# A four-layer decoder trunk on eight cores: phase barriers removed, weights cast by DMA, attention placed inside the convolution, down-projection fused with the embedding

## The chip, the cores and the metric

One Trainium2 chip, eight cores. Each core runs the same program on one of eight sequences of 4096 tokens; there is no traffic between cores. The metric is the device time of the slowest core in microseconds (us). The chip has two dies, cores 0 to 3 and cores 4 to 7. TensorE is the engine that runs the matmuls; ScalarE, VectorE and GpSimd do the work element by element; PSUM is the memory that matmuls write to, SBUF the one that tiles lie in. An execution can fall into a slower state, in which the cores of one die or of both show a lower granted TensorE clock (the changed kernel's run of 10,140.83 us: 0.968 to 0.969 on cores 0 to 3, 0.983 to 0.985 on cores 4 to 7); runs are compared within one state, and where an experiment was run on a chip that was seldom in the fast state, its stages are compared on cores whose clock was not lowered (how, is told with the experiments).

## The reference

Four layers, width 1024, and a last RMS norm. One layer, cut to what matters:

```python
a = rms_norm(h, norm_mix_g[i])
z = a @ w_in[i]                          # 7936 columns: q, k, v, conv x/B/C, gating u|v, three gates
q, k = rotary_partial(zq), rotary_partial(zk)
ya = dilated_mixture(q, k, v)            # 12 heads of 64; three groups of 4 heads with
                                         # (window, dilation) = (128,1), (512,4), (2048,16)
yb = zb * short_conv(zc * zx, conv_w[i]) # causal, width 3
yc = spatial_gating(zs, ...)             # u * (tril(W_s) layer_norm(v) + b), chunks of 128
gates = sigmoid(zg)
m = gates[0]*(ya @ w_branch_a[i]) + gates[1]*(yb @ w_branch_b[i]) + gates[2]*(yc @ w_branch_c[i])
h = h + m @ w_out[i]
h = h + square(relu(rms_norm(h, norm_mlp_g[i]) @ w_up[i])) @ w_down[i]
h = h + sigmoid(rms_norm(h, norm_ple_g[i]) @ w_ple_gate[i]) * (p[i] @ w_ple_proj[i])
```

Attention works in blocks of 128 queries against their own and the previous block of keys of the same residue; the three groups' outputs are weighted by their softmax denominators, so the sum of exponentials is needed as well as the weighted values.

## The kernel before

Activations lie with the channel on the partitions and the token along the row; a tile is 512 tokens. A layer is eight phases, each ended by a wait of all engines for all:

```python
    def barrier(self):
        tot = dict(self.count)
        for e in ENGS:
            for k, v in tot.items():
                # ... every engine waits for the last instruction of every other, and for every DMA
                self.streams[e].append(("w", k, v))
    # ...
    for l in range(nl):
        # ...
        phase_qkv(l, aT, aR, preload=lambda: load_act(aTd, aT, aR, "aTd"))   # activations back from DRAM
        phase_conv_gates(l, aT, aR)
        phase_sgu(l, aT, aR)
        phase_attn(l)
        phase_merge(l, xT if l == 0 else hT, wts)
        phase_ffn_up(l, cT, cR, preload=lambda: load_act(cTd, cT, cR, "cTd"))
        phase_ffn_down(l, wd, rwd)
        phase_ple(l, wg, wp, rwp, m, fuse)
```

Weights come as f32 into a staging buffer and are cast to bf16 by ScalarE and VectorE in turn. Attention puts the mask into PSUM by matmuls and makes the denominators by matmuls against ones:

```python
    for (mi, ksl, vbi) in kbs:
        for ps in (psE, psO):
            e.matmul(ps[:, mi * 256:(mi + 1) * 256], lhsT=ident, rhs=maskb[:, mi, 0:256], start=True, stop=False, ...)
    # ... scores of 128 columns on top; exponential on ScalarE; then per head
            ins = e.matmul(pso[pb:pb + 64, ...], lhsT=vs[:, vbi, j * 64:(j + 1) * 64], rhs=pt[:, c0:c0 + 128], ...)
            ins = e.matmul(pso[pb:pb + 64, 256 + ...], lhsT=onesb[:, 0:64], rhs=pt[:, c0:c0 + 128], ...)
```

In the merge, the output projection of a tile follows that tile's own products and GpSimd additions. Norms of a tile are written to DRAM and read back by the next phase.

The softmax here doesn't subtract the row's maximum and nothing guards it: scores larger than these inputs give would overflow.

Of the kernel before, what the change touches and what calls it, by code (L numbers as in the profile page):

```python
# [13 lines left out]
AX = mybir.AxisListType  # L14
# [3 lines left out]
T = 512  # L18
NT = S // T
KC = D // 128  # L20
NL = 4
INW = 7936
DFF = 4096
PLE = 256
# [3 lines left out]
MASKV = -240000.0  # L28
# [3 lines left out]
C_G = 4864  # L32

ENGS = ("pe", "act", "dve", "pool", "sp")
DBG = 99

class Res:
    __slots__ = ("writers", "readers", "excl")

    def __init__(self):  # L40
        self.writers = {}
        self.readers = {}
        self.excl = False

class Prog:
    def __init__(self, nc):
        self.nc = nc
        self.streams = {e: [] for e in ENGS}
        self.count = {e: 0 for e in ENGS}
        self.seen = {e: {} for e in ENGS}  # L50
        self.semh = {}
        self.res = {}
        self.ndma = 0

    def R(self, *key):
        r = self.res.get(key)
        if r is None:
            r = self.res[key] = Res()
        return r

    def newsem(self, key):
        self.count[key] = 0
        return key

    def _deps(self, eng, reads, writes):
        deps = {}
        for r in reads:
            for k, v in r.writers.items():
                if deps.get(k, 0) < v:
                    deps[k] = v  # L70
            if r.excl:
                for k, v in r.readers.items():
                    if k != eng and deps.get(k, 0) < v:
                        deps[k] = v
        for w in writes:
            for dct in (w.writers, w.readers):
                for k, v in dct.items():
                    if k != eng and deps.get(k, 0) < v:
                        deps[k] = v
# [20 lines left out]
    def dma(self, out, in_, sem, reads=(), writes=(), q="sp"):  # L100
        self._deps(q, reads, writes)
        self.count[sem] += 16
        v = self.count[sem]
        self.streams[q].append(("o", lambda e, o=out, i=in_: e.dma_start(out=o, in_=i), sem, 16))  # L104
# [5 lines left out]
        self.ndma += 1  # L110

    def barrier(self):
        tot = dict(self.count)
        for e in ENGS:
            seen = self.seen[e]
            for k, v in tot.items():
                if k == e and e == "pe":
                    continue
                if v > 0 and seen.get(k, 0) < v:
                    self.streams[e].append(("w", k, v))  # L120
                    seen[k] = v
        for r in self.res.values():
            r.writers = {}
            r.readers = {}
# [37 lines left out]
class Arena:  # L162
    def __init__(self, nc, limit=229000):
        self.nc = nc
        self.off = 16640
        self.n = 0
        self.limit = limit

    def alloc(self, shape, dtype, name="t"):
        esz = 4 if dtype in (F32, I32) else 2  # L170
        nbytes = esz * int(np.prod(shape[1:]))
        nbytes = (nbytes + 63) // 64 * 64
        off = self.off
        self.off += nbytes
        assert self.off <= self.limit, ("SBUF arena overflow", name, self.off)
        self.n += 1
        return self.nc.alloc_sbuf_tensor_at("%s_%d" % (name, self.n), list(shape), dtype, offset=off)

    def mark(self):
        return self.off  # L180

    def reset(self, m):
        self.off = m

def build_program(nl=NL, final_norm=True, stop=99):
    nc = bass.Bass("TRN2", target_bir_lowering=False)
    P = Prog(nc)
    A = Arena(nc)
# [7 lines left out]
    xT = din("xT", [D, S])  # L196
    pT = din("pT", [NL, PLE, S])
    pos = din("pos", [1, S], I32)
    w_in = din("w_in", [NL, D, INW])
    w_a = din("w_a", [NL, 768, D])  # L200
    w_b = din("w_b", [NL, 512, D])
    w_c = din("w_c", [NL, 512, D])
    w_out = din("w_out", [NL, D, D])
    w_up = din("w_up", [NL, D, DFF])
    w_down = din("w_down", [NL, DFF, D])
    w_pg = din("w_pg", [NL, D, D])
    w_pe = din("w_pe", [NL, PLE, D])
    sgwT = din("sgwT", [NL, 4, 128, 128])
    gains = din("gains", [128, NL * 3 + 1, KC])
    convw = din("convw", [128, NL, 4, 3])  # L210
    lng = din("lng", [NL, 1, 512])
    lnb = din("lnb", [NL, 1, 512])
    sgb = din("sgb", [NL, 1, 512])
    cmat = din("cmat", [128, 4, 128])
    cmask = din("cmask", [128, 2, 512])
    invf = din("invf", [128, 1])
    outT = nc.dram_tensor("outT", [D, S], F32, kind="ExternalOutput").ap()

    hT = dscr("hT", [D, S], F32)
    cosD = dscr("cosD", [128, S], F32)  # L220
    sinD = dscr("sinD", [128, S], F32)
    qkT = dscr("qkT", [12, 128, S], BF16)
    Vd = dscr("Vd", [3, 128, 32 * 256], BF16)
    ybT = dscr("ybT", [4, 128, S], BF16)
    ycT = dscr("ycT", [4, 128, S], BF16)
    gT = dscr("gT", [24, 128, S], BF16)
    yaT = dscr("yaT", [6, 128, S], BF16)
    fT = dscr("fT", [32, 128, S], BF16)
    cTd = dscr("cTd", [KC, 128, S], BF16)
    aTd = dscr("aTd", [KC, 128, S], BF16)  # L230

    PS = [nc.alloc_psum_tensor("ps%d" % i, [128, 512], F32) for i in range(8)]
    PSR = [P.R("ps", i) for i in range(8)]
    for r_ in PSR:
        r_.excl = True

    cm = A.alloc([128, 4, 128], BF16, "cm")
    ident, rotT, onesb, trilb = (cm[:, i, :] for i in range(4))
    cmf = A.alloc([128, 4, 128], F32, "cmf")
    onesf = cmf[:, 2, :]  # L240
    maskb = A.alloc([128, 2, 512], BF16, "maskb")
    gsb = A.alloc([128, NL * 3 + 1, KC], F32, "gsb")
    cwsb = A.alloc([128, NL, 4, 3], F32, "cwsb")
    invfsb = A.alloc([128, 1], F32, "invf")
    epsb = A.alloc([128, 1], F32, "epsb")
    Rconst = P.R("const")
    base_mark = A.mark()

    cnt = {"sem": 0}

    def dsem():
        cnt["sem"] += 1
        key = "d%d" % cnt["sem"]
        if key not in P.count:
            P.newsem(key)
        return key

    _pbar = P.barrier

    def barrier():  # L260
        _pbar()
        cnt["sem"] = 0

    P.barrier = barrier

    class Slots:
        def __init__(self, n, shape, dtype, name):
            self.t = [A.alloc(shape, dtype, name) for _ in range(n)]
            self.r = [P.R(name, id(self), i) for i in range(n)]
            self.s = [dsem() for _ in range(n)]  # L270
            self.i = -1
            self.n = n

        def next(self):
            self.i = (self.i + 1) % self.n
            return self.t[self.i], self.r[self.i], self.s[self.i]

    psrot = {}

    def next_ps(lo=0, hi=8):  # L280
        i = psrot.get((lo, hi), lo)
        psrot[(lo, hi)] = lo + (i + 1 - lo) % (hi - lo)
        return PS[i], PSR[i]

    def setup():
        m = A.mark()
        s0 = dsem()
        mf = A.alloc([128, 2, 512], F32, "mf")
        P.dma(cmf[:], cmat, s0, writes=[Rconst])
        P.dma(mf[:], cmask, s0, writes=[Rconst])  # L290
        P.dma(gsb[:], gains, s0, writes=[Rconst])
# [1039 lines left out]
```

## Time and profile before

Median 12,855.75 us of the first three runs (12,852.4 to 12,867.8). The table by stage that the prediction shows (the second layer of core 3) gives 3156 us for a layer, of which TensorE is busy 2549.6.

A window minus its busy time is TensorE standing still: 606 us a layer. The clock records of that core add a second cost that the busy column hides: for 644 us of the layer, idle time included, the granted clock was 0.5 of full. Besides 1 and 0.5 these records hold one more value, 0.8125 (0.81 in the profile's views): 472 us of core 3's whole run, none of it in that layer. The texts call stretches at 0.81 the limit or the limiter, and stretches at 0.5 half clock or cold; the words stand for the granted clock alone. One row of the groups shows what the attention spends on its mask. The columns are line, engine, operation, output and inputs, shape, count, busy us and mean ns, idle time before and who ended it:

```profile
L839 PE MATMUL ps<-maskb_45,cm_43 128*128 128x256 bf16 x1368 | 275.9, 332 | 221.9 <-DMA ks_114<-qkT 64.6
```

1368 matmuls in four layers are 342 a layer, 37 us at the 109 ns of a full-rate matmul of 256 columns and 69 us as they ran.

### The profile page before, as it was taken

To read this page: it belongs to the slowest core of one execution; us is meant where nothing else is said; L and a number is where in the kernel's file an instruction comes from. 1 tells how busy PE (TensorE), PEld (TensorE's weight loads), DVE (VectorE), ACT (ScalarE), POOL (GpSimd) and SP (SyncE) were. 2 spreads that over 40 slices of the span, in tenths; PEclk is the share of its full clock that TensorE was granted. 3 is DMA by queue.
4 is the path that set the end of the run, shared out by engine and by line. 5 is a ranking of instruction groups with operands and counts; after the bars stand their busy time and mean duration, and the time that the engine had idled before them with its cause. 6 is when DMAs were issued, how large, how long until landed. Compare 5 with 4: busy or idle time off the path is not lost.

```text
span 12831.0 us, 145503 instructions; the slowest of 8 cores (12743.4 to 12831.0 us)
## 1 busy us (share of the span) xinstructions
PE 10312.1 (80%) x53288; PEld 4828.8 (38%) x53288; DVE 4763.2 (37%) x7023; ACT 3613.4 (28%) x5176; POOL 523.0 (4%) x360
## 2 busy tenths in 40 slices
PE   4995587897799468799679956789968995788996
PEld 1542333443254243344235423334424432333442
DVE  5513363313640336331473044632155304463215
ACT  2232502302323251320332334132043223413204
POOL 0001020000000102000000010100000001010000
PEclk8997698998899779999889968999989986799998
DMA  3230365343423136534332314553343221455443
GB/s 124 80 110 31 131 208 166 132 171 129 144 74 115 53 135 207 166 136 158 126 133 79 115 48 155 188 168 143 139 144 129 78 97 48 152 185 170 142 144 125
DMA packets 1066742, 1660.73 MB, mean 129 GB/s; under 512 B 25536, under 2 KB 801728, under 8 KB 1016512
## 3 DMA queue, kind: packets, MB, share of 16 engines
q1 hardware_dynamic: 1066048, 1651.42, 38.0%
q8 instruction: 442, 7.24, 0.2%
q14 instruction: 252, 2.06, 0.1%
HBM read 1017.98 MB, written 633.34 MB: 129 GB/s over the span
## 4 chain that ended last, share of the span: by engine, by line
PE 60%; DMA 12%; DVE 12%; issue 6%; ACT 5%; POOL 2%; SPq 2%; DVEq 0%; ACTq 0%; POOLq 0%
PE ps L515 28%; PE ps L1098 14%; PE ps L1027 4%; PE ps L591 3%; PE ps L1001 3%; DMA bgstg_50<-w_down 2%; SPq L104 2%; PE ps L451 2%; DMA bgstg_51<-w_down 2%; PE ps L846 1%; PE ps L839 1%; PE ps L875 1%; PE ps L1168 1%; PE ps L728 1%; PE ps L880 1%
## 5 line engine op out<-in xcount | busy, mean ns | idle before, releaser
L839 PE MATMUL ps<-maskb_45,cm_43 128*128 128x256 bf16 x1368 | 275.9, 332 | 221.9 <-DMA ks_114<-qkT 64.6
L515 PE MATMUL ps<-aT_395,wcg_414 128*128 128x512 bf16 x1152 | 277.9, 408 | 12.9 <-DMA wstg_413<-w_in 12.9
L515 PE MATMUL ps<-aT_395,wcg_415 128*128 128x512 bf16 x1152 | 280.2, 410 | 7.1 <-DVE wcg_415 L361 7.1
L515 PE MATMUL ps<-cT_138,wup_141 128*128 128x512 bf16 x1024 | 234.6, 391 | 51.8 <-DMA cT_138<-cTd 33.1
L515 PE MATMUL ps<-cT_471,wup_474 128*128 128x512 bf16 x1024 | 235.3, 392 | 45.4 <-DMA cT_471<-cTd 31.4
L515 PE MATMUL ps<-cT_360,wup_363 128*128 128x512 bf16 x1024 | 232.4, 389 | 43.6 <-DMA cT_360<-cTd 29.1
L515 PE MATMUL ps<-aT_284,wcg_303 128*128 128x512 bf16 x1152 | 253.0, 381 | 12.7 <-DMA wstg_302<-w_in 12.7
L515 PE MATMUL ps<-aT_173,wcg_192 128*128 128x512 bf16 x1152 | 252.2, 381 | 13.3 <-ACT wcg_192 L359 13.3
L515 PE MATMUL ps<-aT_58,wcg_81 128*128 128x512 bf16 x1152 | 252.6, 381 | 12.2 <-ACT wcg_81 L359 12.2
L515 PE MATMUL ps<-cT_249,wup_252 128*128 128x512 bf16 x1024 | 227.5, 383 | 40.1 <-DMA cT_249<-cTd 29.9
L515 PE MATMUL ps<-aT_284,wcg_304 128*128 128x512 bf16 x1152 | 252.3, 381 | 7.8 <-DVE wcg_304 L361 7.8
L515 PE MATMUL ps<-aT_58,wcg_82 128*128 128x512 bf16 x1152 | 252.3, 381 | 7.4 <-DVE wcg_82 L361 7.4
L515 PE MATMUL ps<-aT_173,wcg_193 128*128 128x512 bf16 x1152 | 252.3, 381 | 7.4 <-DVE wcg_193 L361 7.4
L1098 PE MATMUL ps<-fs_150,wd_137 128*128 128x512 bf16 x1024 | 223.2, 381 | 29.8 <-DMA fs_150<-fT 29.8
L1098 PE MATMUL ps<-fs_261,wd_248 128*128 128x512 bf16 x1024 | 224.4, 382 | 27.6 <-DMA fs_261<-fT 27.6
L1098 PE MATMUL ps<-fs_372,wd_359 128*128 128x512 bf16 x1024 | 224.4, 382 | 23.7 <-DMA fs_372<-fT 23.7
L515 PE MATMUL ps<-cT_249,wup_253 128*128 128x512 bf16 x1024 | 229.3, 386 | 15.9 <-ACT relu_257 L1063 6.9
L1098 PE MATMUL ps<-fs_483,wd_470 128*128 128x512 bf16 x1024 | 223.2, 381 | 22.3 <-DMA fs_483<-fT 22.3
L515 PE MATMUL ps<-cT_471,wup_475 128*128 128x512 bf16 x1024 | 230.6, 388 | 12.8 <-ACT relu_479 L1063 6.1
L515 PE MATMUL ps<-cT_360,wup_364 128*128 128x512 bf16 x1024 | 227.0, 384 | 15.9 <-ACT relu_368 L1063 7.1
L515 PE MATMUL ps<-cT_138,wup_142 128*128 128x512 bf16 x1024 | 227.1, 384 | 15.5 <-ACT relu_146 L1063 9.0
L839 PEld LDWEIGHTS ps<-maskb_45,cm_43 128*128 128x128 bf16 x1368 | 117.6, 109 | 290.7 <-issue 251.4
(969 smaller groups left out, 20599.0 us busy)
## 6 DMA issues: line engine op xcount, KB each, us to landing
bgstg_50<-w_down SPq DMA_DIRECT2D x32, 1024.0 KB, 10.0
bgstg_51<-w_down SPq DMA_DIRECT2D x32, 1024.0 KB, 7.2
fT<-frow_143 SPq DMA_DIRECT2D x16, 1024.0 KB, 4.3
fT<-frow_144 SPq DMA_DIRECT2D x16, 1024.0 KB, 5.1
fs_150<-fT SPq DMA_DIRECT2D x16, 1024.0 KB, 12.9
fs_151<-fT SPq DMA_DIRECT2D x16, 1024.0 KB, 12.4
fT<-frow_254 SPq DMA_DIRECT2D x16, 1024.0 KB, 4.9
fT<-frow_255 SPq DMA_DIRECT2D x16, 1024.0 KB, 5.0
```

The lines of the kernel that those rows point to most:

```text
L104: self.streams[q].append(("o", lambda e, o=out, i=in_: e.dma_start(out=o, in_=i), sem, 16))
L451: ins = e.matmul(ps[:], lhsT=onesb, rhs=sq[:, c, :], start=(c == 0), stop=(c == KC - 1))
L515: ins = e.matmul(ps[:ncols, :], lhsT=wt[:, kc, col0:col0 + ncols], rhs=actT[:, kc, t * T:(t + 1) * T], start=(kc == 0), stop=(kc == kcn - 1))
L591: ins = e.matmul(ps[:, 0:256], lhsT=aT[:, kc, t0:t0 + dil * 127 + 1:dil], rhs=wt[:, kc, :], start=(kc == 0), stop=(kc == KC - 1))
L728: ins = e.matmul(ps[:], lhsT=aT[:, kc, b * 128:(b + 1) * 128], rhs=wv[:, kc, :], start=(kc == 0), stop=(kc == KC - 1))
L839: e.matmul(ps[:, mi * 256:(mi + 1) * 256], lhsT=ident, rhs=maskb[:, mi, 0:256], start=True, stop=False, skip_group_check=True)
L846: ins = e.matmul(ps[:, c0:c0 + 128], lhsT=ks[pb:pb + 64, jj, ksl], rhs=qs[pb:pb + 64, jj, qsl], start=False, stop=True, skip_group_check=True)
L875: ins = e.matmul(pso[pb:pb + 64, pr_ * 128:(pr_ + 1) * 128], lhsT=vs[:, vbi, j * 64:(j + 1) * 64], rhs=pt[:, c0:c0 + 128], start=(i == 0), ...
L880: ins = e.matmul(pso[pb:pb + 64, 256 + pr_ * 128:256 + (pr_ + 1) * 128], lhsT=onesb[:, 0:64], rhs=pt[:, c0:c0 + 128], start=(i == 0), stop ...
L1001: ins = e.matmul(ps[:], lhsT=wt[:, kc, oc * 128:(oc + 1) * 128], rhs=yt[:, k0 + kc, :], start=(kc == 0), stop=(kc == kn - 1))
L1027: ins = e.matmul(ps[:], lhsT=wo[:, kc, oc * 128:(oc + 1) * 128], rhs=mT[:, kc, :], start=(kc == 0), stop=(kc == KC - 1))
L1098: ins = e.matmul(ps[:], lhsT=wd[:, kc, oc * 128:(oc + 1) * 128], rhs=ft[:, kc, :], start=(kc == 0), stop=(kc == 31))
```

## The change

The intent is that TensorE never stops: no stage waits for the end of another, every stage starts its weights ahead, and stages with little TensorE work are put inside stages with much.

- No barriers. Stages are generators, interleaved by the order in which they are drawn; only true dependences wait.
- Weights go straight from f32 in DRAM to bf16 in SBUF by DMAs issued from GpSimd.
- Tiles of 256 tokens. The norm of the mixer writes the next layer's resident activations, that of the MLP the resident input of the up-projection: no way through DRAM.
- Attention is token-major: the values carry a 65th column of ones, so one matmul yields values and denominator; the mask is a bf16 product on VectorE. One attention unit is issued with each convolution group. Division and transposition back happen inside the gates stage.
- Gating: layer norm by the statistics instruction, gain and bias folded behind the spatial product.
- Merge: output projection one tile late. Down: the embedding of the tile before runs inside the down-projection of the present one.
- The additions of the rotary embedding go from VectorE to GpSimd.

The diff has 2,600 lines; its core:

```diff
-            P.dma(st[:, 0:kn, 0:cn], src3[...], ss, writes=[sr])            # f32 staging, then ACT or DVE casts
+        P.dma("pool", dst_ap, src_ap, reads=reads, writes=[t.r], max_dma_last_dim=8192)   # the DMA casts
 ...
-                for (mi, ksl, vbi) in kbs:                                  # mask into PSUM, per key block
-                    for ps in (psE, psO):
-                        e.matmul(ps[...], lhsT=ident, rhs=maskb[:, mi, 0:256], start=True, stop=False, ...)
+                        ins = e.matmul(ps4[:, j, kb], lhsT=kt[ki_][:, j, kblk * 128:(kblk + 1) * 128],
+                                       rhs=q[:, j, :, b * 128:(b + 1) * 128], start=True, stop=True)
+            act(o, i_, AF.Exp, pr, [pt.r], scale=0.125)
+            tt("dve", o, o, m, ALU.mult, [pt.r, maskb.r], [pt.r])
+                        ins = e.matmul(ps[:, j * 65:(j + 1) * 65], lhsT=pt[:, j // 2, kb, j % 2, :],
+                                       rhs=vv[n][:, kblk, j, :], start=(n == 0), stop=(n == len(kbs) - 1))
 ...
-        phase_conv_gates(l, aT, aR)
-        phase_sgu(l, aT, aR)
-        phase_attn(l)
+        for _ in gb:                       # one attention unit ...
+            next(cv, None)                 # ... and one convolution group
+        drain(cv)
 ...
+            merge(t, 0)                    # merge of tile t
+            merge(t, 1)
+            # ...
+                wout(t - 1, 0)             # output projection of tile t - 1
+                wout(t - 1, 1)
 ...
+                    down(t, q, o)          # down-projection of tile t
+                    if t > 0:
+                        if k == 2:
+                            nrm_e(t - 1)
+                        if k in (6, 7, 8, 9):
+                            ple(t - 1, k - 6)      # embedding of tile t - 1
+                        if k == 11:
+                            nrm_n(t - 1)           # next layer's activations of tile t - 1
```

## The prediction

> **What bounds the kernel now.** I read the page's summary first, then the chain that ended last, then a table of busy times by stage for the second layer, then the rows behind the worst stages.
>
> ```profile
> PE 10312.1 (80%) x53288; PEld 4828.8 (38%) x53288; DVE 4763.2 (37%) x7023; ACT 3613.4 (28%) x5176; POOL 523.0 (4%) x360
> ...
> PEclk8997698998899779999889968999989986799998
> ...
> PE 60%; DMA 12%; DVE 12%; issue 6%; ACT 5%; POOL 2%; SPq 2%; DVEq 0%; ACTq 0%; POOLq 0%
> ```
>
> TensorE is the only engine over half busy, yet only 60% of the ending chain is TensorE's: the other 40% is TensorE waiting for something. By stage (layer 2; from top to bottom q/k/v, convolution and gates, spatial gating, attention, merge, up, down, per-layer embedding):
>
> ```profile
> core 3: us, PE busy (x) PEld busy (x) DVE busy (x) ACT busy (x) POOL busy (x), PEclk, DMA share, GB/s
> ...
> 3312.00:3660.00 348.00, 281.63 (x1640) 166.57 (x1640) 191.63 (x300) 107.89 (x201) 0.00 (x0) 0.91 0.36 124
> 3660.00:4196.00 536.00, 501.42 (x2304) 225.84 (x2304) 116.25 (x172) 151.10 (x237) 0.10 (x1) 0.97 0.28 94
> 4196.00:4476.00 280.00, 143.25 (x640) 64.67 (x640) 122.94 (x163) 77.25 (x98) 37.48 (x16) 0.73 0.09 33
> 4476.00:4757.00 281.00, 180.60 (x2394) 110.95 (x2394) 87.57 (x128) 183.74 (x313) 0.00 (x0) 0.76 0.37 135
> 4757.00:5202.00 445.00, 353.68 (x1504) 151.06 (x1504) 251.47 (x384) 41.41 (x25) 83.80 (x64) 0.90 0.63 198
> 5202.00:5689.00 487.00, 444.99 (x2016) 198.24 (x2016) 184.97 (x272) 176.72 (x271) 0.00 (x0) 0.97 0.43 143
> 5689.00:6150.00 461.00, 444.90 (x2048) 200.98 (x2048) 46.60 (x67) 5.08 (x4) 0.00 (x0) 0.98 0.42 150
> 6150.00:6468.00 318.00, 199.18 (x760) 79.84 (x760) 163.73 (x246) 145.84 (x138) 9.38 (x8) 0.81 0.44 142
> ```
>
> The stages add to 3156 us a layer. Up, down and gates are full and at full clock; spatial gating, attention, merge and embedding are not full, and their clock is low as well (0.73 to 0.90). So a gap costs twice. The price of a full-rate matmul stands in the chain in order of time, and the price of a starved one, with the POOL row that starves it, in the groups:
>
> ```profile
> 405.15 83.85 PE ps L591 x768
> ...
> 664.84 345.51 PE ps L515 x1600
> ```
>
> ```profile
> L1027 PE MATMUL ps<-mT_241,wo_221 128*128 128x512 bf16 x512 | 128.7, 418 | 39.4 <-POOL mT_241 L1012 39.4
> ...
> L1012 POOL TENSOR_TENSOR mT_241<-mt_201_243,mt_205_247 128x512 bf16<-128x512 f32 x32 | 43.2, 1349 | 67.0 <-DVE mt_201_243 L1010 67.0
> ```
>
> 345.51/1600 = 216 ns for 512 columns, 83.85/768 = 109 ns for 256 columns: halving the width loses nothing. The starved output projection takes 128.7/512 = 251 ns.
>
> [...] 0.73 and 0.76 in the stages full of gaps, 0.97 in full ones. [...] the same 60 us of gates on core 3 and core 5:
>
> ```profile
> 10330.00:10390.00 60.00, 60.00 (x238) 25.24 (x237) 1.23 (x1) 17.70 (x30) 0.00 (x0) 0.84 0.28 97
> ...
> 10330.00:10390.00 60.00, 60.00 (x280) 27.18 (x278) 1.23 (x1) 22.48 (x36) 0.00 (x0) 1.00 0.32 106
> ```
>
> [...] plain 2 MB loads of this kernel land in 8.0 us, 260 GB/s. [...] The trace has contiguous POOL additions only, 2.35 us for 1024 columns.
>
> **The change part by part.** All TensorE times are counts times 109 or 216 ns; for matmuls of 128 columns or less I take 90 ns, an estimate from the gating product's groups of four, which take 0.58 us with 0.31 us for one: (0.58-0.31)/3.
>
> (1) q/k/v. 768 matmuls of 256 and 864 of 512 columns stay: 84+187 = 271 us against 348. Gone: the copy of the activations back from DRAM (26 to 30 us of wait), weight casts, the barrier. New: each 1024-column rotary addition goes to POOL, with stepped reads in two of three head groups.
>
> (2) Attention inside the convolution. A unit (96 of them) has 4 score matmuls of 256 (0.44 us), 8 value matmuls of 65 columns (0.72; the 65th column is the denominator, so mask and denominator matmuls vanish) and one convolution group of 8x216 ns (1.73): 2.89 us, 277 in all. ACT needs per unit an exponential of 1024 (1.06, from 128x1024 rows), a 260-column copy (0.38) and a third of a 0.6 us copy: 1.6 us. DVE needs the mask product (at most 1.2) and a third of four 0.69 us operations: 2.1 us. Both hide under 2.89.
>
> (3) Spatial gating: 8 tiles x (64x216 ns + 16x90 ns) = 122 us against 280. DVE goes to bn_stats and per-partition scalars, some 10 us a tile, under the 15.3 of TensorE.
>
> (4) Gates 1536x216 ns = 332, plus 192 transposes, 17: 349. Convolution, gates and attention were 536+281 = 817; now 277+349 = 626.
>
> (5) Merge in 256-token tiles: 184 matmuls x 109 ns x 16 = 321 us against 445. The output projection now runs one tile late, so POOL's additions (eight of 1.27, 10 us a tile) lie under 20 us of matmuls. The traffic is 4.5 MB in 20 us, 225 GB/s, near the 198 of before, in larger rows.
>
> (6) Up: 442 against 487; the wait for w_down and the activations goes.
>
> (7) Down with the embedding of the tile before: 352x109 ns x 16 = 615 against 461+318 = 779. The norm chain (table load 1.28, two ACT steps 0.8, eight DVE steps 3.2, from half of the 0.67 us rows plus overhead: about 5.4 us) lies behind four down groups of 1.75 us.
>
> Sum: 271+277+122+349+321+442+615 = 2397 us a layer, 9588 for four. First norm and tables, 16 loads of 1 MB at about 5 us, less the value matmuls woven in, and the last tile: 95. That is 9683 with TensorE never waiting, which it will not reach. I add per layer, by judgement: 20 for the POOL additions in (1), 15 in attention, 12 in gating (sqrt's table loads), 20 for weights that come late, 15 each for merge, down and joints: 112, or 448. Result **10,130 us**, 21% below before. TensorE does almost the same work (9588 of warm time against 10312 busy, part of it at half clock); what goes is waiting and cold clock.
>
> **The rivals.** (a) The clock limit. If the denser kernel held the limiter on everywhere, 9588/0.8125 = 11,800, about 12,350 in all: still 4% faster. Against it: whole 450 us stretches of down run at 0.97 to 0.99 on all eight cores, and the page's clock averages 0.89 only through gaps. A millisecond of limit costs 0.19 ms; I allow up to two.
> (b) The cast queue becomes the wait. One POOL queue carries all weights in order. In the gates stage three blocks lie ready, 3x29 us of work (349/12 each); after 29 us, 11.5 MB of merge weights are put into the queue ahead of the fourth block's 1 MB: 12.5 MB in 58 us, 215 GB/s needed. In up, 4.2 MB of w_down goes ahead of a 1 MB block due two blocks of 27.6 us later: 5.2 MB in 55 us, 95 GB/s, four times. At 100 GB/s the first loses 125-58 = 67 us a layer and the second nothing: +270, about 10,400. At 50 GB/s they lose 192 and four times 49: +390 a layer, about 11,700. For it: the change has no other queue for weights[...]. Against: 260 GB/s of the plain loads, if the cast does not slow them.
> (c) POOL bounds q/k: [...] at twice, 32 units lose 0.8 us each, +105 us in four layers.
> (d) Waits return as small ones, since the tiles are half as long: 2 us in every tile of (5) and (7) is 2x16x2x4 = 256 us, more with cold clock. [...] Against: each chain has two or more groups of slack.
>
> **Range and chances.** Without (a) to (d), 9,850 (the 448 cut to a third); with (b) at 100 GB/s and (c), or with (d) and some of the limiter, 10,500 to 10,600. I take 9,850 to 10,600 for 8 in 10. Slower than before would need a stall of 2.7 ms[...]: 2%. Faster by over 2%: 0.97, within: 0.01, slower: 0.02.
>
> **What would show it.** TensorE about 95% busy and over 90% of the ending chain; clock 0.97 or more outside the limiter's stretches; a layer near 2500 us; q/k with TensorE full or behind POOL (c); gates and up with waits for weights (b); no clock of 0.5 inside merge and down. If the layer exceeds 2700 us with the clock at 1.0, a stage's overlap has failed and my sum is wrong there; if the clock is 0.81 for milliseconds, (a) is what I undersized.

## The result, and the profile after

The changed kernel took 10,087.74 us (median of four runs: 10,029.06, 10,034.66, 10,140.83, 10,154.73), against 12,854.08 us (four runs of before). The ratio of the fast runs is 0.783, with a 95% interval of 0.778 to 0.789; a ratio is the mean time of one kernel's fast runs over that of the other's of the same rounds, so it is not quite the ratio of the two medians. The result is right by the reference. The two slower of the four runs had a clock of 0.968 to 0.974 on one die or both, the two faster ones 0.982 to 0.985.

The page of the changed kernel (10,029 us, all eight cores at 0.983 to 0.985); the same three lines as the prediction shows of before:

```profile
PE 9482.4 (95%) x65256; PEld 6243.0 (62%) x65804; DVE 4257.7 (42%) x6179; ACT 3118.1 (31%) x4128; POOL 1791.9 (18%) x1362
...
PEclk8999999999999999999999999999999999999999
...
PE 82%; DVE 4%; DMA 4%; ACT 3%; issue 3%; POOL 3%; SPq 0%; DVEq 0%; ACTq 0%; POOLq 0%
```

TensorE went from 80% to 95% of a shorter span, the row of digits of the clock has lost its sevens and sixes, and of the chain that ended last TensorE now has 82% instead of 60%. TensorE is busy 830 us less, although it issues 12,000 more (and narrower) matmuls.

By stage, layer 2 of core 6. First the 170 us until the value matmuls run without a break, then the values, q and k, convolution with attention, gating, gates, merge, up, and down with embedding:

```profile
core 6: us, PE busy (x) PEld busy (x) DVE busy (x) ACT busy (x) POOL busy (x), PEclk, DMA share, GB/s
0.00:170.00 170.00, 66.02 (x368) 45.62 (x368) 69.35 (x152) 55.62 (x67) 7.07 (x12) 0.84 0.60 174
2599.00:2701.00 102.00, 96.46 (x864) 90.92 (x865) 15.88 (x30) 39.66 (x65) 2.11 (x4) 0.98 0.38 118
2701.00:2899.00 198.00, 187.99 (x849) 84.33 (x865) 118.10 (x96) 49.76 (x49) 162.17 (x61) 0.99 0.33 100
2899.00:3138.00 239.00, 226.87 (x1766) 130.42 (x1796) 151.53 (x229) 136.92 (x224) 68.11 (x75) 0.98 0.57 158
3138.00:3296.00 158.00, 128.26 (x614) 58.41 (x624) 75.60 (x150) 55.42 (x57) 17.84 (x17) 0.92 0.16 43
3296.00:3655.00 359.00, 345.34 (x1710) 162.60 (x1746) 59.28 (x199) 121.49 (x129) 10.05 (x15) 0.98 0.59 159
3655.00:3970.00 315.00, 314.56 (x2875) 280.91 (x2875) 222.66 (x236) 52.87 (x91) 162.89 (x128) 1.00 0.67 226
3970.00:4429.00 459.00, 449.53 (x2081) 207.69 (x2120) 167.57 (x148) 134.07 (x135) 15.43 (x24) 0.99 0.46 118
4429.00:5061.00 632.00, 609.05 (x5535) 538.83 (x5533) 236.44 (x421) 177.63 (x271) 8.46 (x16) 1.00 0.35 110
```

| | before us | after us | saved us |
|---|---|---|---|
| q, k, v | 348 | 300 | 48 |
| convolution, attention, gates | 817 | 598 | 219 |
| spatial gating | 280 | 158 | 122 |
| merge | 445 | 315 | 130 |
| up | 487 | 459 | 28 |
| down and embedding | 779 | 632 | 147 |
| layer | 3156 | 2462 | 694 |

Of these 694 us a layer, 502 are idle time of TensorE (606 became 104, from window minus busy) and 192 busy time. Time at half clock in that layer went from 644 to 61 us, so a good part of what the busy column lost is matmuls that no longer run at half speed (how much was not measured apart from the matmuls that were left out). What TensorE still waits for in this layer (line waited in, the releaser, us in total, times, longest):

```profile
PE psall L853 <- ACT ut_214_256 L396: 12.5, 4, 4.0
PE psall L853 <- ACT ut_215_257 L396: 12.1, 3, 4.2
PE psall L959 <- ACT grow_227_269 L396: 11.6, 2, 8.7
PE psall L1290 <- DVE tmd_286_328 L399: 10.9, 15, 0.7
```

L853 is the gating's first product (v): 25 us in seven waits, the longest of 4.2 us. L959 is the gates, with one long wait of 8.7 us. What stands behind that one is in the chain in order of time (start, us, what):

```profile
3308.55 29.21 DMA gD<-grow_227_269
3337.85 1.03 ACT grow_227_269 L396
```

The store of the first gate rows took 29 us. At this place the program asks for the four weight blocks of the merge, 11.5 MB of f32. Only three of them, 7.3 MB, go into the cast queue at once: the fourth goes into the place of a gating tile, and its issue waits for that tile's store (engine, destination, releaser, us in total, times, longest):

```profile
POOL wo_284 L109 <- DMA yD<-yc_217_259: 28.5, 1, 28.5
```

So the store of the gates ran beside 7.3 MB of casts, which landed within some 30 us; the prediction and the expectation of b2 reckon with 11.5. The timeline of 4 us of the convolution stage shows one unit of attention and convolution (start, us, engine, line, operation):

```profile
2960.17 0.41 PE L752 MATMUL psall<-vtt_234,pt_185_227 128*128 128x65 bf16 x8
...
2960.41 0.60 PE L727 MATMUL psall<-qz_235,kt_233 128*128 128x256 bf16 x4
...
2960.85 1.89 PE L391 MATMUL psall<-aT_185,wcv_223 128*128 128x512 bf16 x8
```

Eight value matmuls of 65 columns take 0.41 us from first start to last end. Over the whole trace the starts of such matmuls follow each other at 29 ns (median of 2,736), those of 128 columns at 56, of 256 at 109, of 512 at 216.

### The profile page after: what moved, and what is told of

It is laid out like the page before. It is cut to its first block, busy times and chain, and to the rows that moved or that the text cites. A ratio compares the mean times of both kernels' runs of the same rounds, so it can differ in the third digit from the quotient of the medians.

```text
span 10027.5 us, 172472 instructions; the slowest of 8 cores (9986.4 to 10027.5 us)
## 1 busy us (share of the span) xinstructions
PE 9482.4 (95%) x65256; PEld 6243.0 (62%) x65804; DVE 4257.7 (42%) x6179; ACT 3118.1 (31%) x4128; POOL 1791.9 (18%) x1362
## 4 chain that ended last, share of the span: by engine, by line
PE 82%; DVE 4%; DMA 4%; ACT 3%; issue 3%; POOL 3%; SPq 0%; DVEq 0%; ACTq 0%; POOLq 0%
PE psall L1144 18%; PE psall L1236 16%; PE psall L959 11%; PE psall L1049 8%; PE psall L391 7%; PE psall L1290 5%; PE psall L1073 4%; PE psall L604 4%; PE psall L537 3%; PE psall L853 2%; ACT L396 2%; PE psall L727 1%; PE psall L1280 1%; PE psall L752 1%; DMA gD<-grow_95_137 1%
## 5 line engine op out<-in xcount | busy, mean ns | idle before, releaser
L1144 PE MATMUL psall<-cT_558,wup_568 128*128 128x512 bf16 x751 | 168.9, 383 | 7.4 <-DVE cT_558 L402 6.3
L1144 PE MATMUL psall<-cT_162,wup_172 128*128 128x512 bf16 x751 | 168.4, 383 | 7.4 <-DVE cT_162 L402 6.3
L1144 PE MATMUL psall<-cT_426,wup_436 128*128 128x512 bf16 x751 | 167.9, 382 | 7.2 <-DVE cT_426 L402 6.3
L1144 PE MATMUL psall<-cT_294,wup_304 128*128 128x512 bf16 x751 | 167.9, 382 | 7.2 <-DVE cT_294 L402 6.3
L1290 PE MATMUL psall<-eT_543_585,wpg_577 128*128 128x256 bf16 x1024 | 127.2, 279 | 20.0 <-DVE tmd_549_591 L399 14.9
L1144 PE MATMUL psall<-cT_558,wup_569 128*128 128x512 bf16 x628 | 138.3, 379 | 0.6
L1144 PE MATMUL psall<-cT_162,wup_173 128*128 128x512 bf16 x628 | 138.3, 379 | 0.6
L1144 PE MATMUL psall<-cT_294,wup_305 128*128 128x512 bf16 x628 | 138.3, 379 | 0.6
L1144 PE MATMUL psall<-cT_426,wup_437 128*128 128x512 bf16 x628 | 138.3, 379 | 0.6
L1144 PE MATMUL psall<-cT_558,wup_575 128*128 128x512 bf16 x627 | 138.1, 379 | 0.7
L1144 PE MATMUL psall<-cT_162,wup_179 128*128 128x512 bf16 x627 | 138.1, 379 | 0.7
L1144 PE MATMUL psall<-cT_294,wup_311 128*128 128x512 bf16 x627 | 138.1, 379 | 0.7
L1144 PE MATMUL psall<-cT_426,wup_443 128*128 128x512 bf16 x627 | 138.1, 379 | 0.7
L1290 PE MATMUL psall<-eT_148_190,wpg_181 128*128 128x256 bf16 x1024 | 123.6, 274 | 15.7 <-DVE tmd_154_196 L399 15.7
L1290 PE MATMUL psall<-eT_280_322,wpg_313 128*128 128x256 bf16 x1024 | 122.2, 272 | 15.9 <-DVE tmd_286_328 L399 15.9
L1290 PE MATMUL psall<-eT_412_454,wpg_445 128*128 128x256 bf16 x1024 | 122.2, 272 | 15.9 <-DVE tmd_418_460 L399 15.9
L1144 PEld LDWEIGHTS psall<-cT_558,wup_568 128*128 128x128 bf16 x768 | 75.7, 99 | 98.1 <-issue 10.4
L1144 PEld LDWEIGHTS psall<-cT_162,wup_172 128*128 128x128 bf16 x768 | 75.6, 99 | 97.8 <-issue 9.9
L1144 PEld LDWEIGHTS psall<-cT_426,wup_436 128*128 128x128 bf16 x768 | 75.5, 98 | 97.2 <-issue 9.0
L1144 PEld LDWEIGHTS psall<-cT_294,wup_304 128*128 128x128 bf16 x768 | 75.5, 98 | 97.2 <-issue 8.9
L959 PE MATMUL psall<-aT_60,wg_135 128*128 128x512 bf16 x501 | 116.4, 389 | 12.6 <-ACT grow_95_137 L396 10.6
```

Source lines behind the costliest of these rows:

```text
L959: ins = e.matmul(ps[:, i * 512:(i + 1) * 512], lhsT=w[:, kc, o2 * 128:(o2 + 1) * 128], rhs=aT[:, kc, c0:c0 + 512], start=(kc == 0), stop=( ...
L1144: ins = e.matmul(ps[:, i * 512:(i + 1) * 512], lhsT=w[:, kc, o2 * 128:(o2 + 1) * 128], rhs=cT[:, kc, c0:c0 + 512], start=(kc == 0), stop=( ...
L1290: ins = e.matmul(ps[:, o2 * T:(o2 + 1) * T], lhsT=w_g[:, kc, oc * 128:(oc + 1) * 128], rhs=eT[:, kc, :], start=(kc == 0), stop=(kc == KC - 1))
```

## The experiments

Twelve kernels ran. They ran on three chips on which the slow state was the rule: the kernel before took 12,776 to 14,200 us there. So I read each experiment by stage: a stage lasts from the first matmul with its first operand to the first matmul of the next stage, in each of eight cores and the first three layers, and only those are kept in which the clock records show no value of 0.81, the clock of the prediction's rival (a) (0.5% of the stage at most). "Stage time" below is the median of the kept ones. The measure holds across chips: in the eight experiments that leave it alone, the up-projection takes 459.2 to 459.9 us against 459.8 in the changed kernel's own profile, and the merge 314.1 to 314.8 against 314.2. The changed kernel's stage times in this measure: values 101.4, q/k 197.2, convolution with attention 237.4, gating 158.5, gates 357.4, merge 314.2, up 459.8, down with embedding 632.9; sum 2459.

My theory was that what the change gained is waiting and cold clock taken out by overlap (attention under convolution, embedding under down, output projection under the next tile), with barriers a smaller part. The first rival: the barriers were the main cost. The second: less TensorE work is the gain. The third: what is left is bound by the cast queue.

### a1: the barriers back

```diff
+    def barrier(self):           # every engine waits for all that was issued so far
+        ...
         drain(g1a)
+        P.barrier()              # and at six further joints of a layer
```

> One part undone: at the seven joints of a layer (before the values, before the gating, before the gates, before and after the merge, after the up-projection, after the down-projection) every engine waits for every other, 28 times in all. My theory: the joints of the changed kernel are worth what a drain and a refill of the pipeline take, some 8 to 15 us each as the joints of the kernel before took, so 60 to 105 us a layer and 220 to 420 us in all: about 10,300 to 10,450 us. The rival, that the barriers were the main cost of the kernel before (what was said first of the change), would have most of the 500 us of idle time a layer come back: over 11,000 us.

Measured: right result; 2515.5 us a layer, plus 56.7, that is 8.1 us a joint. The die whose clock stayed at 0.974 to 0.975 took 10,197 to 10,243 us, against 9,986 to 10,028 of the changed kernel. The time came in the values (+14), q/k (+13), up (+13) and gates (+7), the rest +10. It is just below the range of my theory, and far from the rival. Put back into the changed kernel, barriers cost about a twelfth of the 694 us a layer; what the kernel before would gain by losing its own, each with the loads that start only behind it, was not run.

### a2 and a2b: attention before the convolution

```diff
-        for _ in gb:
-            next(cv, None)
-        drain(cv)
+        drain(gb)                # all attention units first
+        for _ in cv:             # then all convolution groups
+            step()               # (a2b only)
```

> One part undone: the 96 attention units of a layer run first and the 96 convolution groups after them, with the same instructions. My theory: alone, a unit is bound by the exponential (1.03 us on ScalarE) with the copy of its values (some 0.4 us) on the same engine, about 1.45 us against 0.85 us of TensorE work, so TensorE idles some 0.6 us in each of 96 units, and runs at the half clock in part of them: the stage grows from 239 us to 300 to 370 us, plus 240 to 500 us in all. The rival, that four units' buffers in flight are enough for attention to run by itself at TensorE's rate: under 20 us a layer.

The first run had a fault of mine: the convolution's stores were held back until after the stage, so that they stored overwritten rows; its result was wrong. The stage took 338.9 us. The corrected kernel:

> The attention ahead of the convolution once more, now with the convolution's stores issued as they fall due; in the first run they were held back, which made its result wrong. If those stores had no part in the time, the stage takes 339 us a layer again (within 5 us) on cores with the limiter off, 101 us more than the changed kernel, and some 79 us of it at the half clock. If the held stores had hidden or caused a wait, it differs by more.

Measured in a2b: right result, stage 358.7 us, plus 121 us a layer, of it 92 us at half clock (the changed kernel: 6). The profiled run, fast on both dies, took 10,506 us. So the first theory's 300 to 370 held, but the second expectation missed: with the stores issued in time the stage is 20 us longer than without. What TensorE waits for in layer 3 of core 6:

```profile
PE psall L752 <- ACT ub L396: 62.4, 83, 8.7
PE psall L391 <- DVE us L399: 9.7, 1, 9.7
PE psall L727 <- ACT pt L396: 8.1, 1, 8.1
```

83 times in 96 units the value product waits for ScalarE's copy of the values before it, which shares ScalarE with the exponential, and in five places that copy itself had waited for a store of earlier values to DRAM (29.3 us in all, the longest 8.2). The convolution's 1.89 us per unit therefore hides two things: ScalarE's second job, and most of the store.

### a3 and a3b: embedding after the whole down-projection

```diff
         for t in range(NT):
             for q in range(4):
                 for o in range(4):
                     down(t, q, o)
-                    # nrm_e, ple, nrm_n of tile t - 1 at fixed places
+            P.dma("sp", hD[t], h[:], ...)       # residual stored
+        for t in range(NT):                     # embedding pass with norms one tile ahead and behind
+            for o in range(4):
+                ple(t, o)
+                ...
```

> One part undone: the down-projection of all 16 tiles first, the residual stored; then the embedding pass in tiles of its own, with its norms, pipelined over tiles. My theory: the embedding pass by itself has too little TensorE work a tile (some 5 us of matmuls) for its chain of square, sum, root, norm, gate, sigmoid and product (10 us or more), so that it is bound by ScalarE and VectorE and goes cold: the two stages together grow from 632 us to 700 to 750 us, plus 280 to 480 us in all. The rival, that only the TensorE work counts, which is the same: within 10 us a layer.

Measured: 945.6 us instead of 632.9, and a wrong result, again by a fault of mine (a buffer of squares was overwritten by the next tile). Mended:

> The run of the same intent before it gave a wrong result by a fault of mine: the next norm of a tile read a buffer of squares that the following tile had begun to overwrite, and so also waited for that tile. Here the squares have two buffers. On cores where the limiter was off, the two stages took 946 us a layer there instead of 633. If the fault made the embedding pass serial, the stages now take 760 to 820 us (the kernel before: 779), plus 130 to 190 us a layer, of it over 60 us at the half clock. If a separate embedding pass is that slow in itself, they stay above 900 us. The rival, that only TensorE work counts: within 10 us of 633, as before.

Measured in a3b: right result, 916.6 us, of it 246 at half clock; the border to the next stage moves with it (values 85 instead of 101), so a layer loses 268 us. The fast run took 11,097 us. The expected 760 to 820 was wrong; the second branch ("that slow in itself") holds. Layer 2 of core 6, the stage's window, and then its waits:

```profile
4697.00:5613.90 916.90, 690.23 (x5628) 578.46 (x5626) 249.97 (x439) 212.95 (x266) 9.01 (x17) 0.87 0.34 113
```

```profile
PE psall L1291 <- DVE tmd L399: 209.2, 45, 7.3
```

The chain in one tile of the pass, by the timeline:

```profile
5353.95 1.28 ACT L396 ACT_TABLE_LOAD   x1
...
5356.25 1.28 ACT L396 ACT_TABLE_LOAD   x1
5356.33 4.60 DVE L402 SCALAR_TENSOR_TENSOR eT<-hd,gsb,rsd 128x256 bf16<-128x256 f32 x8 [3.18 <-ACT rsd L396]
...
5361.68 3.57 PE L1291 MATMUL psall<-eT,wpg 128*128 128x256 bf16 x16 [6.83 <-DVE tmd L399]
```

The product that frees the PSUM bank (tmd) stands in VectorE's queue behind eight norm instructions (4.6 us), these behind two ScalarE steps between two table loads. TensorE stands 6.8 us, twice in a tile, and comes back at half clock: sixteen matmuls in 3.57 us instead of 1.91. The kernel before ran this pass in 512-token tiles, with twice the TensorE work to each such chain: 318 us. With 256-token tiles the fusion is not a bonus: down and a separate embedding pass, as I built it, take 901 us (917 less the 16 of the moved border), 122 more than the same two stages of the kernel before.

### a4: every score matmul twice

```diff
+                        for _ in range(2):
                             ins = e.matmul(ps4[:, j, kb], lhsT=kt[ki_][...], rhs=q[...], start=True, stop=True)
```

> One cost doubled: each score matmul of the attention is issued twice into the same place (same result). If TensorE bounds the convolution with attention, as I hold, the stage grows by the time of those matmuls, 0.43 us for each of 96 units = 41 us a layer, 164 us in all. If ScalarE or VectorE bounds it (exponential 1.03 us and copies, mask product 0.69 us and evictions), under 10 us a layer.

Measured: right result; the stage takes 269.7 instead of 237.4, plus 32.3 us a layer, in ten kept stages from 269.3 to 270.5. That is four fifths of the 41 us; the rest went into the 12 us that the stage stood idle. TensorE bounds the stage, with about 0.1 us of slack a unit. The other stages did not move.

### a5: the output projection right after its own tile

```diff
-            # wout(t - 1, ...) between merge(t, 1) and merge(t, 3), nrm(t - 1) after merge(t, 3)
+            if t > 0:
+                nrm(t - 1)           # ahead of merge(t, 2)
             ...
             merge(t, 3)
+            if t < NT - 1:
+                for o in range(4):
+                    wout(t, o)
```

> One part undone: in the merge, the output projection of a tile follows its own products at once, instead of one tile later. My theory: TensorE then waits in each of 16 tiles for the last product on VectorE (1.75 us) and the two additions on GpSimd (1.3 us each), some 4.5 us, and part of the matmuls after it run at the half clock: 314 us a layer become 385 to 425. The rival, that the four groups of lead inside the tile suffice: under 330.

Measured: right result; the merge takes 472.7 instead of 314.2, plus 158 us a layer, with 145 us at half clock. The direction is that of my theory, but the wait is twice what I reckoned. The merge of layer 1, core 2:

```profile
PE psall L1073 <- POOL mT L399: 126.7, 15, 9.1
```

```profile
1322.07 6.24 DVE L402 SCALAR_TENSOR_TENSOR cT<-hm,gsb,rsm 128x256 bf16<-128x256 f32 x8
...
1328.23 3.42 DVE L399 TENSOR_TENSOR prd<-psall,gm 128x1536 f32<-128x1536 f32 x2
```

8.5 us a tile: I had counted the last product and GpSimd's two additions (4.3 us), but ahead of the tile's last two products VectorE does the eight norm instructions of the tile before (6.2 us), where I had placed them. Work that is not needed now stands before work that is. So the run undoes more than the lag of one tile: what the lag alone is worth was not measured apart from the place of the norm.

### b1: the root of the variance after the groups that it doesn't concern

```diff
-            act(mv[:, :, 2:3], mv[:, :, 1:2], AF.Sqrt, ...)     # ahead of u's two Gelus
-            ... reciprocal, vb
             for i in range(2):                                  # u's groups and Gelus
                 ...
+            act(mv[:, :, 2:3], mv[:, :, 1:2], AF.Sqrt, ...)
+            ... reciprocal, vb
-                if i == 0 and prev is not None:                     # tail of the tile before: one group later
+                if i == 1 and prev is not None:
                     tail(prev)
```

> A remaining wait taken away: in the spatial gating the root of the variance, with its two table loads, goes to ScalarE after the two groups of u, and the tail of the tile before goes one group later. My theory: the gating is held up by that root, which lies ahead of u's Gelu in ScalarE's queue and keeps both PSUM buffers full, 3.1 us in each of 8 tiles, and a quarter of a tile's matmuls go cold after it: 158 us a layer become 125 to 135. The rival, that the Gelus and the statistics themselves bound the stage: 150 us or more.

Measured: right result; 118.3 us, minus 40 a layer, more than expected. Half-clock time in the stage fell from 25.7 to 3.2 us. In the changed kernel's trace, ScalarE loads a table (1.28 us), takes the root (0.30), loads the other table (1.28), and only then runs the two Gelus that free the PSUM banks. The run moves the root and the tail of the tile before together; they were not tried one by one. The gating of layer 2 on core 2 of this run:

```profile
3079.60:3196.30 116.70, 116.12 (x613) 56.35 (x624) 73.45 (x144) 53.11 (x53) 17.06 (x17) 1.00 0.18 47
```

TensorE is busy 116.1 of 116.7 us. Its busy time fell by 12 us as well, and its work is the same: those 12 were matmuls at half clock.

### b2: the merge's weights asked for one by one

```diff
-            if i in (8, 78):
+            if i in (8, 24, 40, 56, 78):
                 next(g2)
```

> A remaining wait taken away: the merge's four weight blocks (11.5 MB) are not asked for in one go during the gates but one after another. My theory: the store of the first gates took 29 us because of that burst, and TensorE lost 8 to 9 us a layer to it: gates 357 us become 347 to 350, the merge stays at 314. The rival, that the store is slow for its own layout: no change in the gates. A risk: a block that now comes late shows as a wait at the start of the merge.

Measured: right result; gates 344.8 instead of 357.4, minus 12.6 a layer, merge 314.3. The 8.7 us wait is gone from the list of waits, and with it 10 us at half clock. The rival (the store's own layout) falls, since the stores are the same. No block came late.

### b3: every cast twice

```diff
         P.dma("pool", dst_ap, src_ap, reads=reads, writes=[t.r], max_dma_last_dim=8192)
+        P.dma("pool", scratch, src_ap, max_dma_last_dim=8192)   # the same weights, cast again
```

> One cost doubled: every cast of weights is followed by the same cast into a scratch tensor, so GpSimd's queue carries twice the weights. From the 2 MB cast of this trace that landed in some 19 us (220 GB/s of the source), the queue is busy some 190 to 240 us of a layer's 2460, and twice that is still under a fifth; so my theory is that only the bursts lose: plus 20 to 60 us a layer, mostly in the gates and at their end. The rival (b) of the prediction, that the queue is near its limit: over 200 us a layer, with TensorE waiting for weights in up and q/k.

Measured: right result; 2568 us a layer (median of cores 4 to 7, layers 2 and 3; the changed kernel has 2459 in this measure), plus 109; by stage gates +56, up +45, convolution +11, q/k +3. That lies between theory and rival: the queue has slack, but less than I held. How the time is lost is the same in both stages. Up, in the chain in order of time:

```profile
4257.18 32.43 DMA fD<-frow
4292.19 29.70 PE psall L1152 x128
4323.29 1.24 DVE frow L407
4324.59 31.39 DMA fD<-frow
```

The stores of the MLP's rows take 18 to 32 us while the 2 MB blocks of the down weights are cast, against a median of 4.5; TensorE waits for the rows they free. In these two stages no wait for weights is listed; TensorE waits for stores that run beside the casts. So rival (b) of the prediction was nearer than I said, but named the wrong victim. (The doubled cast also writes to DRAM, which the single one does not, so the run overstates the load.)

### b4: the kernel before without its mask

```diff
-                    for (mi, ksl, vbi) in kbs:
-                        for ps in (psE, psO):
-                            e.matmul(ps[...], lhsT=ident, rhs=maskb[...], start=True, stop=False, ...)
-                                           rhs=qs[pb:pb + 64, jj, qsl], start=False, stop=True,
+                                           rhs=qs[pb:pb + 64, jj, qsl], start=True, stop=True,
```

> The kernel before with its mask matmuls left out of the attention (wrong result on purpose): the matmuls that the change removes, alone. My theory: the attention of the kernel before is bound by ScalarE and by waits, not by TensorE (181 us busy of 281), so a layer loses under 10 us. The rival, that less TensorE work in attention is what was gained: a layer loses what those matmuls take, 37 us at full clock and 73 us at half.

The result is wrong on purpose. Measured: from the first to the last matmul on queries, keys and values the attention takes 235 us instead of 256 (medians of the stretches without a clock of 0.81), minus 22. From merge to merge on cores 4 to 7 the median layer is 17 us shorter (3133 against 3149; single layers spread from 3106 to 3148 and from 3134 to 3160), and cores 4 to 7 end at 12,669 to 12,732 us, where undisturbed dies of the unchanged kernel took 12,681 to 12,787 on the two other chips. By the means of these ends it is some 8 us a layer, so whether my 10 us was exceeded is not sure; it is far less than the rival's 37 to 73. In place of the matmuls TensorE idles and runs cold: the share of half clock between those matmuls rose from 0.53 to 0.78. Less TensorE work in a stage that TensorE doesn't bound is worth little; for the mask the second rival falls. The denominators' matmuls against ones, which the change removes too, were not taken out alone.

### c1: three mends together

b1 and b2, and a start in which the first tiles are loaded ahead of the rotary tables and the first norm works two tiles at a time.

```diff
-    setup()                                  # tables for the rotary embedding, then
+    posi = setup()
 ...
-            sq = sqs.next()
-            norm_sq(h, sq)                   # square, sum, root, apply, one tile after the other
+            norm_mm(sq, ps, pr)
+            norm_rstd(ps, pr, rstd)
+            if t + 1 < NT:
+                sq = square(t + 1)           # the next tile's square ahead of this one's apply
```

> Three mends together: the gating order, the spread weights, and a first norm that loads its tiles before the tables and works two tiles at a time. My theory: minus 25 to 33 us a layer in the gating, minus 8 in the gates, minus 60 to 70 at the start: 9,830 to 9,880 us on a core with the limiter off, against 9,987 to 10,028 for the changed kernel. The rival, that these waits only move elsewhere: over 9,950.

Measured: right result. All eight runs fell in the slow state. In two of them die 1 was undisturbed for the whole run (clock 0.991 to 0.992) and its cores took 9,751 to 9,775 us, against 9,986 to 10,028 of the changed kernel's at 0.983 to 0.985 and 12,681 to 12,787 of undisturbed dies of the kernel before: 2.5% and 23% less. Gating is 118.3, gates 344.3, the first value matmul comes after 32 us instead of 60, and the first value stage 158 instead of 171. The start gave 40 us, not 60 to 70; the two others gave more than expected (53 a layer). One of the eight runs took 29,331 us, with mean clocks of 0.31 to 0.81 on six cores, while two cores of the same execution took 9,752 and 9,767; what happened there is open. The whole-chip time of this version in the fast state was not measured; by its cores it beats both kernels.

### What the slow state looks like in these runs

These records show longer stretches at 0.81 than the trace of the kernel before. Two cores of a4, both of die 0 (the first and third windows of three; in the second both are at 0.99):

```profile
core 0: us, PE busy (x) PEld busy (x) DVE busy (x) ACT busy (x) POOL busy (x), PEclk, DMA share, GB/s
0.00:3500.00 3500.00, 3237.13 (x21733) 2061.00 (x21963) 1498.36 (x2246) 1140.84 (x1499) 708.96 (x513) 0.98 0.46 130
...
7300.00:10550.00 3250.00, 3197.82 (x19159) 2042.03 (x19303) 1170.97 (x1711) 855.65 (x1147) 447.65 (x346) 0.81 0.38 110
...
core 2: us, PE busy (x) PEld busy (x) DVE busy (x) ACT busy (x) POOL busy (x), PEclk, DMA share, GB/s
0.00:3500.00 3500.00, 3351.93 (x19229) 2031.95 (x19230) 1302.68 (x1830) 944.09 (x1236) 638.89 (x436) 0.81 0.39 113
...
7300.00:10550.00 3250.00, 3142.39 (x22731) 2169.96 (x22730) 1330.84 (x1952) 988.61 (x1323) 457.03 (x359) 0.99 0.43 126
```

In the windows cores 0 and 1 are at 0.81 from 7,300 to 10,550 us of their span and at 0.98 up to 3,500; cores 2 and 3 are at 0.81 up to 3,500 and at 0.99 from 7,300. Why a core is at 0.81 in one stretch and not in another was not shown. What a stage took in stretches at 0.81, by stage: up 555 us (1.21 times 459.8), merge 377 (1.20), q/k 234 (1.19), gates 418 to 421 (1.17), convolution with attention 276.5 (1.16), down 733.5 (1.16), gating 156 (1.0), and gating in b1 142 (1.20). In the trace of the kernel before, 25 us of core 3 at 0.81 (10,410 to 10,435 us) hold some 96 matmuls of 512 columns, 260 ns each instead of 216 (1.20). Whether a stage slows at 0.81 told here what bounds it: the gating didn't (1.0), since ScalarE held it; after b1 it did (1.20).

## Why the prediction was right

**The sum by stage.** Predicted TensorE time at full rate, measured busy time in layer 2, and the idle time left in the window:

| stage | predicted | busy | idle | judged loss |
|---|---|---|---|---|
| (1) q, k, v | 271 | 284.5 | 15.6 | 20 |
| (2) convolution, attention | 277 | 226.9 | 12.1 | 15 |
| (3) gating | 122 | 128.3 | 29.7 | 12 |
| (4) gates | 349 | 345.3 | 13.7 | 20 (late weights) |
| (5) merge | 321 | 314.6 | 0.4 | 15 |
| (6) up | 442 | 449.5 | 9.5 | |
| (7) down and embedding | 615 | 609.1 | 23.0 | 15 |
| joints | | | | 15 |
| layer | 2397 | 2358.2 | 104.0 | 112 |

The window of (1) holds the embedding of the last tile of the layer before, some 16 us (a3b moved it out: values 85 instead of 101), which the prediction counts under (7). Four layers of 2462 are 9,848; the profiled run took 10,028, so start and end, over the repeating layer, were 180 us where 95 were predicted. The prediction of 10,130 for the median met 10,088, and 10,028 in the profiled run: the terms were off by minus 39 x 4 in work, minus 8 x 4 in losses and plus 85 at the ends, which sum to minus 103. So the closeness of the number is partly luck: two errors cancel. Of the signs that the prediction named, TensorE's share (95%), the clock, the layer and merge and down without half clock came as said; of the chain that ended last TensorE has 82%, not over 90%, and no wait for late weights is listed in gates or up.

**Which terms were mis-sized.** In step (2) the eight value matmuls were put at 90 ns each, from a group of the kernel before; they follow each other at 29 ns, 0.41 us for eight instead of 0.72. The 128-column ones of steps (3) and (4) run at 56 ns. The estimate came from groups of four in a stage of the kernel before that ran at 0.73 of the clock. The trace of the changed kernel has 29, 56, 109 and 216 ns for 65, 128, 256 and 512 columns. With its 29 ns, step (2) comes to 0.44 + 8 x 0.029 + 1.73 = 2.40 us a unit, 231 for the stage (an estimate from these figures); the trace has 227 busy. In the start, what was mis-sized is the serial chain of the first norm, with the first load at 38 us behind the tables; c1 took back 40 of those us.

**Parts of the theory that the runs showed.** That waiting and cold clock, not work, were what the attention of the kernel before lost: b4 removes 37 us of work a layer and gets 8 to 22, by the measure taken. That overlap is what the change lives on: undoing it costs 121 us a layer in the attention, 158 in the merge, 268 in the embedding, each with 90 to 250 us of half clock, against 57 for barriers at all joints. These costs don't add up to the 694 gained, and can't: the undone parts run in half-length tiles, in which each wait weighs more than it did before. That a gap costs twice, by the wait and by the clock after it: in a5, TensorE idles 127 us and the stage grows by 158.

**The rivals.** (a) The clock of 0.81: absent in the profiled run, whose clock records hold 1 and 0.5 alone; two of the four runs (10,141 and 10,155) had mean clocks of 0.968 to 0.974 on one die or both, against 0.982 to 0.985 elsewhere, and on the other chips slow runs were the rule. A layer at 0.81 adds up to 2,871 us by the stages above, so a run at 0.81 throughout would take about 11,700 (an estimate: four such layers and 190 us), where the prediction had 12,350; the cores of c1, a shorter program, whose mean clocks were 0.815 to 0.818 took 11,472 to 11,505. (b) The cast queue: it did become a wait, once a layer, and through the store of the gates, not through late weights: 8.7 us directly, 12.6 with the cold clock (b2). The rate that the prediction could not know: the 2 MB blocks of the down weights, 4.2 MB of f32, land in 17 to 19 us, 220 to 250 GB/s, and the first three blocks of the merge in some 30 us, 245 GB/s: more than the 215 needed in its tightest place. (c) GpSimd in q/k: additions of 2.35 us in the undilated group, 3.72 and 4.14 in the others (58% and 76% more), where the prediction's worse case was twice 2.35. The last exceed the 3.89 us of TensorE a unit by a quarter of a microsecond, for a third of the units: a few us, in place of the judged 20. The longest wait in q/k (5.2 us, releaser DVE) has another cause: for the coming attention VectorE clears two halves of a query tile, 3.47 us each, and the rotary products stand behind them. (d) Small waits: they came in the gating (seven, up to 4.2 us) and in the embedding (under 1 us each, 15 times). The gating is the one judged loss that was clearly too small, 12 against 30 idle and 12 cold; b1 took them away by order alone, with the root moved in ScalarE's queue and the tail moved with it. Step (5) had been given 15 and lost nothing.

**What stays open.** The stage gains of up (28) and q/k/v (48) were not taken apart by an experiment. The way through DRAM of the norms was not put back, nor were the weight casts on ScalarE and VectorE, and no run has tiles of 512 tokens in the new order: these parts of the change have no price of their own.

## What to carry to other kernels

When a stage has less work for the bounding engine than its chain on the other engines is long, put it inside a stage with surplus; shortening the tile makes that more urgent, since the chain shrinks less than the matmuls: here the eight norm instructions of the embedding went from 5.4 us for 512 tokens to 4.6 for 256, and the two table loads stayed at 1.28 each. When a wait is left, read the waiting engine's releaser, then what stands ahead of it in that engine's queue: twice here (root before Gelu, norm before product; in b1 a second move came with it) the cure or the cost was order alone. And here a burst of loads was paid for by what was stored at that moment (29 us instead of 4).
